# A main tile's 128 partitions ordered by batch first in a streaming dot-product and record-count kernel

## The chip, the cores and the metric

The kernel runs on one core of one Trainium2 chip. The metric is the device time of one execution in microseconds (us). The kernel before takes 630.5 us, the median of two runs (630.48 and 630.51 us).

## The reference

```python
def setup_inputs():
    B, S, D = 8, 2048, 4096
    return {
        "x": np.random.randn(B, S, D).astype(np.float32),
        "w": np.random.randn(D, 1).astype(np.float32),
    }

def reference(x, w):
    proj = (x @ w).squeeze(-1)
    cm = np.maximum.accumulate(proj, axis=1)
    is_record = (proj >= cm).astype(np.float32)
    return np.cumsum(is_record, axis=1).astype(np.float32)
```

Each of the 8 x 2048 rows of x (4096 floats, 16 KiB) is reduced to one dot product with w. Along each batch a running maximum is taken, every position that reaches it counts as a record, and the records are counted up. The input x is 268.4 MB; the output is 64 KiB.

## The kernel before, in words

**Tiles.** The sequence is cut into five groups of N = 384 positions and a rest of 128 positions. A group has NT = 6 main tiles. A main tile holds four batches (`b0` is 0 or 4, alternating with the tile number t) and 128 positions: 512 rows of x, 8 MiB. Each of the 128 partitions gets R = 4 consecutive rows, 64 KiB in one piece. In the kernel before partition p = 4q + b holds rows 4q to 4q + 3 of batch b, so that the batches alternate from one partition to the next (L171 to L173, the pattern "q b (r d)"). Three buffers in SBUF take the tiles in turn (`xbuf`, NS = 3).

**Loads.** All loads of x are issued by SyncE (SP), one after another in the order of the loops at L168. Each main tile is one DMA (L185), but for the last tile of the last group, which is two halves (L178 and L181). A load into a used buffer waits until the tile three places earlier has been consumed (`user_before`, `free`). Behind the main tiles come 13 smaller loads for the rest of 128 positions (L207); their source runs "b i d -> i b d", 32 positions outermost and four batches inside. The 16 KiB of w come by one DMA of 8 partitions from ScalarE's queue (L191). Each group's counts leave by a DMA of 8 partitions (L195), the last ones by L434.

**Compute on a main tile.** VectorE takes the first 2816 columns of each of the four rows of every partition with a fused multiply and sum (L125, in the loop at L270). GpSimd multiplies the remaining 1280 columns of all four rows in one instruction (L291), and ScalarE sums them, row by row (L131). When ScalarE has summed the fourth row the buffer is free. After the six tiles of a group GpSimd adds the two partial sums (L295) and multiplies them with a mask of 128 x 4, `by_b`, that tells which of the four batches a partition holds (L298). TensorE then sorts the sums into rows of batches and columns of positions with 12 matmuls (L335), whose right-hand operand is a mask of 128 x 32, `by_i`, that tells which q a partition holds. VectorE runs the scans on the [8, 384] result (L141, L144, L147) at the head of the next group.

**Masks.** `by_b` and `by_i` are made at the start by two reductions over the identity on VectorE (L249, L253). They also serve the rest of 128 positions, whose partitions alternate batches in the same way (L368, L373, L378). The second reduction signals ScalarE by the semaphore `fo`.

The order on each engine is the order of the program text. Nothing is scheduled by a planner.

Of the kernel before, what the change touches and what calls it, by code (L numbers as in the profile page):

```python
# [13 lines left out]
ALU = mybir.AluOpType  # L14
# [6 lines left out]
def kernel(  # L21
# [16 lines left out]
    P = 128  # L38
# [3 lines left out]
    R = 4  # L42
    NS = 3
    H = 4
    Q = P // H
# [22 lines left out]
    def rows_of(m):  # L68
        return m * H % B, m * H // B * Q
# [9 lines left out]
    def sb(shape, name, **kw):  # L79
        return pool.tile(shape, FP32, name=name, **kw)  # L80

    identity = sb([P, P], "identity")
# [6 lines left out]
    cnt = sb([B, N + P], "cnt")  # L89
    gmask = sb([P, R * NC * B], "gmask")  # L90
    masked = sb([P, 10 * B], "masked")
    fold = sb([P, H + Q], "fold")
    w_v = wpool.tile([P, CV], FP32, name="w_v")
    ps = wpool.tile([P, WC], FP32, name="ps")
    w_row = w2[:NW, :WC]
    by_b, by_i = fold[:, :H], fold[:, H:]

    off = [0]

# [22 lines left out]
    V, A, G, T, SY = nc.vector, nc.scalar, nc.gpsimd, nc.tensor, nc.sync  # L122
# [28 lines left out]
    def at(t):  # L151
        return xbuf[t % NS]

    def user_before(g, t):
        return (t - NS, g + 1) if t >= NS else (t + NT - NS, g)

    def free(u, n):
        return (p7, n) if u == NT - 1 else (fr[u], 2 * n)
# [7 lines left out]
    with tc.tile_critical(no_gpsimd_drain=True):  # L166

        for g in range(NG):  # L168
            for t in range(NT):
                b0, s0 = t % 2 * H, STARTS[g] + t // 2 * P  # L170
                src = x[b0 : b0 + H, s0 : s0 + P, :].rearrange(  # L171
                    "b (q r) d -> q b (r d)", r=R
                )  # L173
                half = R // 2 * D
                last = t == NT - 1
                u, n = user_before(g, t)
                if last and g == NG - 1:
                    i = SY.dma_start(  # L178
                        out=at(t)[:, :half], in_=src[:, :, :half]
                    ).then_inc(xs[t], 16)  # L180
                    SY.dma_start(  # L181
                        out=at(t)[:, half:], in_=src[:, :, half:]
                    ).then_inc(xh, 16)
                else:
                    i = SY.dma_start(out=at(t), in_=src).then_inc(xs[t], 16)  # L185
                    if last:
                        SY.sem_inc(xh, 16)
                if n:
                    i._wait_ge(*free(u, n))
                if g == t == 0:  # L190
                    A.dma_start(  # L191
                        out=w_row, in_=w.rearrange("(k c) one -> k (c one)", k=NW)
                    ).then_inc(ws, 16)
                if t == 4 and g:
                    SY.dma_start(  # L195
                        out=out[:, STARTS[g - 1] : STARTS[g]], in_=cnt[:, :N]
                    )._wait_ge(cs, g + 1).then_inc(od, 16)
# [7 lines left out]
        for i, (m, c0, c1, _, _) in enumerate(TILES):  # L205
            u, xb = slot(m)
            d = SY.dma_start(  # L207
                out=xb[:, c0:c1],
                in_=x[
                    rows_of(m)[0] : rows_of(m)[0] + H,  # L210
                    S0 + rows_of(m)[1] : S0 + rows_of(m)[1] + Q, c0:c1,
                ].rearrange("b i d -> i b d"),
            ).then_inc(xq[i], 16)
# [7 lines left out]
            out=identity, in_=identity, compare_op=ALU.not_equal, fill=1.0,  # L221
# [10 lines left out]
        for n, k in enumerate(order):  # L232
# [3 lines left out]
                out=dst, lhsT=identity[:NW, k : k + 1].to_broadcast([NW, P]),  # L236
                rhs=w_row, start=True, stop=True,
# [12 lines left out]
            out=by_b, in_=identity.rearrange("p (i b) -> p b i", b=H),  # L250
            op=ALU.add, axis=mybir.AxisListType.X,
        )._wait_ge(con, 7)
        V.tensor_reduce(  # L253
            out=by_i, in_=identity.rearrange("p (i b) -> p i b", b=H), op=ALU.add,
            axis=mybir.AxisListType.X,
        ).then_inc(fo, 1)
# [7 lines left out]
        def landed(i, t, j):  # L264
            if j == 0:
                i._wait_ge(xs[t], 16)
            elif t == NT - 1 and j == R // 2:
                i._wait_ge(xh, 16)
# [16 lines left out]
        with G.Fori(0, NG):  # L285
            for t in range(NT):
                rows = at(t).rearrange("p (r d) -> p r d", r=R)
                n = R // 2 if t == NT - 1 else R
                for j in range(0, R, n):
                    xl = rows[:, j : j + n, VC:]  # L290
                    i = G.tensor_mul(  # L291
                        out=xl, in0=xl, in1=w_one.to_broadcast([P, n, PC])
                    ).then_inc(pl, 1)
                    landed(i, t, j)
            G.tensor_tensor(  # L295
                out=sum_t, in0=sum_v, in1=sum_p, op=ALU.add
            )._wait_ge(fr[NT - 1], 2).then_inc(mk, 1)
            G.tensor_tensor(  # L298
                out=gmask.rearrange("p (k b) -> p k b", b=H),
                in0=sum_t.rearrange("p (k o) -> p k o", o=1).to_broadcast(  # L300
                    [P, R * NT, H]
                ),
                in1=by_b.rearrange("p (o b) -> p o b", o=1).to_broadcast(
                    [P, R * NT, H]
                ),
                op=ALU.mult,
            )._wait_ge(mk, 1).then_inc(mk, 1)
            G.wait_ge(pg, 1).then_inc(pg, -1)
# [15 lines left out]
        with T.Fori(0, NG):  # L324
            T.wait_ge(mk, 2).then_inc(p7, 1)
            T.sem_inc(mk, -2)
            T.sem_inc(fr[NT - 1], -2)
            for s in (*xs, xh):
                T.sem_inc(s, -16)
            T.sem_inc(pg, 1)  # L330
            T.wait_ge(od, 16).then_inc(od, -16)  # L331
            for j in range(R):
                for c in range(NC):
                    k = j * NC + c
                    i = T.matmul(  # L335
                        out=ps[:B, c * P + j : (c + 1) * P : R],
                        lhsT=gmask[:, k * B : (k + 1) * B],
                        rhs=by_i, start=True, stop=True,
                    )
                    if k == 0:  # L340
                        i.then_inc(pd, 1)
            i.then_inc(psr, 1)
# [48 lines left out]
        for m in range(B - 2):  # L391
            k = m // 2
            v, p = acc_v[:, m : m + 1], acc_p[:, m : m + 1]
# [16 lines left out]
        for i in range(B - 2, len(TILES)):  # L410
            n = i - (B - 2)
            m, p = TILES[i][0], TILES[i][4]
# [55 lines left out]
```

## Time and profile before

| what | value |
| --- | --- |
| median of the runs before | 630.5 us |
| the profiled execution's own time | 630.45 us |
| its span, first to last instruction | 628.3 us |
| VectorE busy | 406.9 us (65%) |
| GpSimd busy | 360.7 us (57%) |
| ScalarE busy | 171.7 us (27%) |
| TensorE busy | 23.2 us (4%) |
| read from HBM | 268.45 MB |
| DMA rate over the span | 427 GB/s |
| a main load, from issue to landing | 41.7 us (median of 29) |

The profile is one execution. Its span leaves out some 2 us at the ends that the time includes. The profile's page gives each engine's busy time, the span cut into 40 equal slices with the busy share of the 16 DMA engines, the DMA queues with their packets, and the chain of waits: the work that ended last, followed back step by step to what released it. An idle engine that isn't on that chain costs nothing.

### The profile page before, as it was taken

What the parts mean: (1) busy time and instruction counts of PE and PEld (TensorE: products, weight loads), DVE (VectorE), ACT (ScalarE), POOL (GpSimd) and SP (SyncE); (2) the same over time, 40 slices, a digit from 0 to 9 for tenths busy, and PEclk for the clock granted to TensorE, in tenths of its full rate; (3) what the DMA queues carried; (4) which work ended last, traced back from release to release, by engine and by line L of the source; (5) the groups of instructions that cost most, each with busy time, mean ns of one, the idle gap of its engine ahead of it and who ended that gap; (6) DMA issues with size and microseconds to landing.
All of it is one profiled execution on the core that took longest, in us unless ns stands there. A gap on an engine that the chain in (4) does not pass through costs nothing.

```text
span 628.3 us, 1242 instructions
## 1 busy us (share of the span) xinstructions
PE 23.2 (4%) x156; PEld 12.7 (2%) x156; DVE 406.9 (65%) x297; ACT 171.7 (27%) x274; POOL 360.7 (57%) x74
## 2 busy tenths in 40 slices
PE   2600000000000000000000000000000000000000
PEld 1200000000000000000000000000000000000000
DVE  0295775567765557865577566676556875559877
ACT  1033302333113333033330313311333202333344
POOL 0264675455764457744467554576445775449585
DMA  9999999999999999999999999999999999999996
GB/s 390 413 455 413 459 409 459 409 459 409 451 417 417 451 409 459 417 451 426 442 455 414 438 430 442 426 455 413 439 430 442 426 455 413 459 397 430 423 428 267
DMA packets 6434, 268.54 MB, mean 427 GB/s; under 512 B 752, under 2 KB 1040, under 8 KB 1568
## 3 DMA queue, kind: packets, MB, share of 16 engines
q1 hardware_dynamic: 6416, 268.50, 98.9%
q14 instruction: 2, 0.02, 0.0%
q10 hardware_dynamic: 16, 0.02, 0.0%
HBM read 268.45 MB, written 0.07 MB: 427 GB/s over the span
## 4 chain that ended last, share of the span: by engine, by line
DMA 71%; POOL 18%; ACT 7%; issue 2%; DVE 1%; SPq 0%; PE 0%
DMA xall<-in_x_dram 71%; POOL xall L291 18%; ACT xall L131 7%; POOL xall L357 1%; DVE xall L125 0%; SPq L185 0%; PE ps L378 0%; ACT masked L373 0%; SPq L207 0%; POOL masked L368 0%; DVE cm L141 0%; DVE cnt L147 0%; DVE ps L144 0%; SPq L463 0%; DVE small L125 0%
## 5 line engine op out<-in xcount | busy, mean ns | idle before, releaser
L125 DVE CUSTOM_DVE_ANT_0 xall<-xall,w_v 128x2816 f32<-128x2816 f32 (+1 forms) x129 | 385.5, 3041 | 167.7 <-DMA xall<-in_x_dram 167.7
L291 POOL TENSOR_TENSOR xall<-xall,w_sb 128x5120 f32<-128x5120 f32 (+1 forms) x35 | 332.2, 9498 | 242.1 <-DMA xall<-in_x_dram 216.8
L131 ACT ACTIVATE xall<-xall 128x1280 f32<-128x1280 f32 (+2 forms) x130 | 161.3, 1241 | 428.3 <-POOL xall L291 411.3
L335 PE MATMUL ps<-fold,gmask 128*8 128x32 f32 x120 | 7.2, 240 | 563.7 <-PEq L331 563.7
L131 ACT ACTIVATION_READ_ACCUMULATOR xall<-xall 128x1 f32 x130 | 24.2, 186 | 0.0
L357 POOL TENSOR_TENSOR xall<-xall,w_sb 128x1280 f32<-128x1280 f32 (+2 forms) x8 | 21.0, 2629 | 4.4 <-DMA xall<-in_x_dram 2.4
L141 DVE TENSOR_TENSOR_SCAN cm<-ps,cm,small 8x384 f32<-8x384 f32 (+2 forms) x9 | 6.9, 765 | 23.6 <-PE ps L335 23.2
L335 PEld LDWEIGHTS ps<-fold,gmask 128*8 128x8 f32 x120 | 6.5, 114 | 565.9 <-issue 565.9
L257 DVE MEMSET ps<- 8x384 f32 x1 | 0.4, 378 | 24.5 <-ACT w L246 24.5
L235 PE MATMUL w_v<-w,identity 8*128 8x512 f32 x14 | 12.2, 1057 | 0.0
L125 DVE DVE_READ_ACCUMULATOR2_ANT small<- 128x1 f32 x133 | 10.8, 81 | 0.0
L295 POOL TENSOR_TENSOR small<-small 128x24 f32<-128x24 f32 x5 | 1.2, 233 | 13.6 <-ACT xall L131 13.6
L147 DVE TENSOR_TENSOR_SCAN cnt<-ps,cnt,small 8x384 f32<-8x384 f32 (+2 forms) x9 | 6.9, 766 | 0.3
L235 PEld LDWEIGHTS w_v<-w,identity 8*128 8x128 f32 x14 | 4.6, 332 | 7.3 <-issue 7.3
L144 DVE TENSOR_TENSOR ps<-ps,cm 8x384 f32<-8x384 f32 (+2 forms) x9 | 3.9, 435 | 0.3
L243 ACT COPY w_sb<-w_v 128x768 f32<-128x768 f32 x1 | 0.8, 798 | 11.4 <-PE w_v L235 11.4
L125 DVE CUSTOM_DVE_ANT_0 xall<-xall,w_v,small 128x480 f32<-128x480 f32 (+2 forms) x4 | 3.1, 811 | 0.2 <-DVE small L125 0.2
L373 ACT ACTIVATE masked<-fold,small 128x4 f32<-128x4 f32 x10 | 3.0, 297 | 0.3
L378 PE MATMUL ps<-fold,masked 128*8 128x32 f32 x20 | 2.0, 234 | 26.2 <-ACT masked L373 18.2
L242 ACT COPY w_sb<-ps 128x512 f32<-128x512 f32 x1 | 0.6, 585 | 8.5 <-PE ps L235 8.5
L368 POOL TENSOR_TENSOR masked<-fold,small 128x4 f32<-128x4 f32 x8 | 1.6, 203 | 1.6 <-DVE small L125 1.6
L235 PE MATMUL ps<-w,identity 8*128 8x512 f32 x2 | 2.1, 1137 | 11.4 <-DMA w<-in_w_dram 11.4
(20 smaller groups left out, 10.0 us busy)
## 6 DMA issues: line engine op xcount, KB each, us to landing
xall<-in_x_dram SPq DMA_DIRECT2D x6, 2048.0 KB, 31.6
xall<-in_x_dram SPq DMA_DIRECT2D x2, 4096.0 KB, 36.6
xall<-in_x_dram SPq DMA_DIRECT2D x1, 1264.0 KB, 34.0
xall<-in_x_dram SPq DMA_DIRECT2D x1, 816.0 KB, 36.6
xall<-in_x_dram SPq DMA_DIRECT2D x1, 784.0 KB, 35.2
xall<-in_x_dram SPq DMA_DIRECT2D x2, 240.0 KB, 26.2
xall<-in_x_dram SPq DMA_DIRECT2D x29, 41.7
xall<-in_x_dram SPq DMA_DIRECT2D x1, 416.0 KB, 37.0
```

What stands on the lines that cost most here:

```text
L125: return V.tensor_tensor_reduce(out=xsl, in0=xsl, in1=wsl, scale=1.0, scalar=seed, op0=ALU.mult, op1=ALU.add, accum_out=dst,)
L131: return A.activation(out=xsl, in_=xsl, func=ACTF.Copy, accum_out=dst)
L141: V.tensor_tensor_scan(out=cm_, data0=src, data1=low, initial=cm0, op0=ALU.max, op1=ALU.max,)._wait_ge(psr, base).then_inc(psr, 1)
L144: V.tensor_tensor(out=src, in0=src, in1=cm_, op=ALU.is_ge)._wait_ge(psr, base + 1).then_inc(psr, 1)
L147: V.tensor_tensor_scan(out=cnt_, data0=src, data1=low, initial=cnt0, op0=ALU.add, op1=ALU.max,)._wait_ge(psr, base + 2).then_inc(cs, 1)
L235: i = T.matmul(out=dst, lhsT=identity[:NW, k : k + 1].to_broadcast([NW, P]), rhs=w_row, start=True, stop=True,).then_inc(bw, 1)
L291: i = G.tensor_mul(out=xl, in0=xl, in1=w_one.to_broadcast([P, n, PC])).then_inc(pl, 1)
L335: i = T.matmul(out=ps[:B, c * P + j : (c + 1) * P : R], lhsT=gmask[:, k * B : (k + 1) * B], rhs=by_i, start=True, stop=True,)
L357: G.tensor_mul(out=xl, in0=xl, in1=w_pool(*p))._wait_ge(xq[i], 16).then_inc(pl, 1)
L368: return eng.tensor_tensor(out=e, in0=by_b, in1=acc.to_broadcast([P, H]), op=ALU.mult)
L373: return A.activation(out=e, in_=by_b, func=ACTF.Copy, scale=acc)._wait_ge(pa, na).then_inc(ms, 1)
L378: return T.matmul(out=ps[:B, k * Q : (k + 1) * Q], lhsT=masked[:, n * B : (n + 1) * B], rhs=by_i, start=start, stop=stop,)
```

## The change

The source pattern of a main tile becomes "b q (r d)": batch outermost, then q, then the 64 KiB piece. Partition p = 32b + q now holds rows 4q to 4q + 3 of batch b. Two further masks, `in_b` (128 x 4) and `in_q` (128 x 32), tell batch and q in this order; two reductions more on VectorE make them at the start, and the mask of a group (L298) and the right-hand operand of its matmuls (L335) use them in place of `by_b` and `by_i`. The loads of the rest of 128 positions, their masks, and all sizes and waits stay as they were.

```diff
-    fold = sb([P, H + Q], "fold")
+    fold = sb([P, 2 * (H + Q)], "fold")
...
-    by_b, by_i = fold[:, :H], fold[:, H:]
+    by_b, by_i = fold[:, :H], fold[:, H : H + Q]
+    in_b, in_q = fold[:, H + Q : 2 * H + Q], fold[:, 2 * H + Q :]
...
                 src = x[b0 : b0 + H, s0 : s0 + P, :].rearrange(
-                    "b (q r) d -> q b (r d)", r=R
+                    "b (q r) d -> b q (r d)", r=R
                 )
...
         V.tensor_reduce(
+            out=in_b, in_=identity.rearrange("p (b q) -> p b q", b=H), op=ALU.add,
+            axis=mybir.AxisListType.X,
+        )
+        V.tensor_reduce(
+            out=in_q, in_=identity.rearrange("p (b q) -> p q b", b=H), op=ALU.add,
+            axis=mybir.AxisListType.X,
+        )
+        V.tensor_reduce(
             out=by_i, in_=identity.rearrange("p (i b) -> p i b", b=H), op=ALU.add,
             axis=mybir.AxisListType.X,
         ).then_inc(fo, 1)
...
-                in1=by_b.rearrange("p (o b) -> p o b", o=1).to_broadcast(
+                in1=in_b.rearrange("p (o b) -> p o b", o=1).to_broadcast(
...
-                        rhs=by_i, start=True, stop=True,
+                        rhs=in_q, start=True, stop=True,
```

## The prediction, written before the changed kernel ran

> **What bounds the kernel now.** I read the page's slices and its DMA part first, then the chain of waits, then a window over three tiles in the steady part.
>
> ```profile
> span 628.3 us, 1242 instructions
> ...
> DMA  9999999999999999999999999999999999999996
> ...
> DMA packets 6434, 268.54 MB, mean 427 GB/s; under 512 B 752, under 2 KB 1040, under 8 KB 1568
> ...
> q1 hardware_dynamic: 6416, 268.50, 98.9%
> ...
> q10 hardware_dynamic: 16, 0.02, 0.0%
> ```
>
> The 16 DMA engines are busy in every slice but the last. The loads of x are the bound, and all of them are on one queue.
>
> Pieces of the chain of waits, in order of time (start us, us, what):
>
> ```profile
> 42.97 11.06 POOL xall L291
> 54.03 0.02 issue
> 54.05 0.04 ACT xall L131
> 54.10 1.13 issue
> 55.23 3.95 ACT xall L131 x7
> 59.18 0.02 issue
> 59.20 41.71 DMA xall<-in_x_dram
> 100.91 0.07 issue
> 100.98 11.06 POOL xall L291
> ```
>
> This is one buffer's round: load, GpSimd, ScalarE, load again, 58.01 us, and it carries three tiles. The chain shows GpSimd in it, but the DMA engines don't stop meanwhile, as the window over that round shows (columns: stretch, length, busy us of each engine, clock, DMA share, GB/s):
>
> ```profile
> core 0: us, PE busy (x) PEld busy (x) DVE busy (x) ACT busy (x) POOL busy (x), PEclk, DMA share, GB/s
> 43.00:101.00 58.00, 0.00 (x0) 0.00 (x0) 36.35 (x25) 15.75 (x26) 33.13 (x4) 1.00 1.00 434
> ```
>
> A DMA share of 1.00 at 434 GB/s: while one tile is consumed, two others are queued. Each engine moves 434/16 = 27.1 GB/s. A tile has 128 pieces of 64 KiB, 8 per engine; three tiles in 58.01 us make 2.417 us a piece. The 30 main tiles take 240 x 2.417 = 580.1 us. All else in the span (first bytes, the smaller loads, the last scans) is 628.3 - 580.1 = 48.2 us.
>
> **What the page tells of how a load is spread.** Every engine that takes part in a DMA ends its share with a small packet. The kernel has 31 main loads and 13 smaller ones into 128 partitions, 5 stores of 8 partitions and w's load of 8. 44 x 16 + 5 x 8 + 8 = 752, the page's count under 512 B. The queue of w's load, q10, has 16 packets: 8 rows and 8 endings. So the loads into 128 partitions run on 16 engines and those of 8 rows on 8 only.
>
> **What the Trainium skill says.**
> - "DMA: Bandwidth & Descriptors", section "Why a DMA increments its semaphore by 16 and not by 1": the number of engines k is the largest up to 16 that divides the slowest dimension (of size over 1) of both source and destination, and on SP's queue these are the lowest-numbered k. The counts above agree: 128 against 32 gives 16, 8 against 8 gives 8.
> - The same page, "Rules for kernel authors": an outermost dimension of size c under 16 confines the whole DMA to at most c engines. No load of before shows a c of 4.
> - The same page, "The descriptor swizzle": a 128-partition transfer on 16 engines gives each one the 8 partitions of one SBUF port. The even 27.1 GB/s per engine fits.
> - "SBUF — State Buffer", section "Door 1: The DMA port swizzle (why `[64,N]` ≈ `[32,N]`)": 16 ports of 8 partitions; partition p and p + 32 share a port, p and p + 64 don't. A port is worth 27.2 GB/s, and partitions 0 to 63 reach 196 GB/s where 0 to 127 reach 328 (1 MiB). No stretch of before has two streams held to one port, so the trace is silent on it.
>
> **The change part by part.**
>
> 1. *Two reductions more on VectorE.* L249 took 377 ns and L253 277 ns: 0.65 us in all. Behind them VectorE sits idle 24.5 us for ScalarE's copy of w (L257), so nothing is added there. The signal `fo` comes 0.65 us later to ScalarE, which then waits 8.5 us for TensorE. If the cover were gone: 0.65 us.
> 2. *Other masks in L298 and L335.* The same shapes and counts, 5 instructions of 345 ns and 120 of 240 ns: 0.
> 3. *The 31 main loads.* The pieces stay 64 KiB and 128 per tile, with the same bytes, issues and waits. What changes is the slowest dimension of the source: 32 (q) becomes 4 (b). With a destination of 128 the largest common k is 4. Engine e then takes batch e, 32 pieces in place of 8, into partitions 32e to 32e + 31; 12 engines get nothing. Whether an engine gets faster when others rest, no stretch of before shows; 10% would be the most I could argue from rates that stand so still, and I keep 27.1 GB/s, since one figure for all sixteen at once speaks for a limit of each engine's own path. Main pieces per engine: 30 x 32 = 960, at 2.417 us: 2320.4 us, in place of 580.1.
> 4. *The ports.* Engine 0 walks partitions 0 to 31 and engine 1 walks 32 to 63, from the same moment, at the same speed: p and p + 32, the same port, all the way. Likewise engines 2 and 3. If a port is worth one engine's rate, each pair shares 27.1 GB/s and a piece takes 4.834 us: 960 x 4.834 = 4640.8 us. What the pair gains is its stagger: the leader enters the next port (4 pieces, 262 KB) alone. In the trace's packet records the first sixteen pieces of before start within 0.42 us of each other, 11 KB or 4% of a port's stretch. With fair sharing the stagger is kept and doesn't grow. It gives back 4% of the second 2320.4: 93 us.
> 5. *Who waits.* SP's loads wait for ScalarE to free a buffer (435.5 us in 22 waits at L185 now). GpSimd's 11.06 us and ScalarE's 5.1 us per tile stay; two tiles of over 77 us each are queued meanwhile, so these hide, and engines 0 to 3 never run dry. w's load has rows on engines 0 to 3 behind slower pieces: some us later, but the first tile itself lands over 50 us later still.
> 6. *The 13 smaller loads* keep 32 outermost and 16 engines. Engines 4 to 15 do their share early; engines 0 to 3 do theirs behind the main pieces, the same bytes per engine as now. The 48.2 us stay.
>
> Sum of the likeliest case, against the profiled execution: 4640.8 - 93 + 48.2 = 4596 us of span. The time stood 2.15 us above the span (630.45 against 628.3), and the median of the runs at 630.5: 4598 us, say 4600.
>
> **Rivals.**
>
> *Four engines, but no collision* (the port isn't the limit, or unfair sharing soon pulls a pair apart by 4 pieces, after which each has a port to itself): 2320.4 + 48.2 + 2.15 = 2371 us. For it: w's eight rows (q10) wrote to partitions 0 to 7 while x streamed to the same ports, and in the packet records they took 84 ns each and the pieces beside them at most 30 ns more than usual. Against it: 2 KB may vanish in a buffer, and the skill's table of ports. Chance 0.28.
>
> *Collision for part of the run* (the stagger grows slowly until the pair is apart): between the two; half of the run makes about 3485 us. Chance 0.15.
>
> *The loads keep 16 engines* (the rule doesn't apply to this form: the split is taken from the 128 partitions, or the two outer dimensions are cut anew). Then part 3 falls, only the hidden 0.65 us is left, and the time is 630.5 us, not slower. It turns on one thing: whether the generator looks at the source's slowest dimension. For it: the two sides of before differ (128 and 32) and still gave 16, so the counts alone don't prove that the smaller rules. Against it: the rule names both sides. Chance 0.04.
>
> *A third limit*: four streams whose addresses lie 32 MiB apart slow one another in HBM. Nothing in the trace shows it, since batches with that distance are read now at 434 GB/s. It would lie above 4720 or, without the ports, between 2400 and 3000; chance 0.02.
>
> **How the numbers follow.** Collision all the way has 0.51, and is the forecast: 4600 us. Its own range runs from 4250 (a stagger of 15 to 20% of a port's stretch) to 4720 (no stagger, and some lost time). With the partial case 0.66 is held. To leave out no more than 2 in 10 the range must reach the no-collision case, which is narrow, at 2371. So 2330 to 4720. About 2% is what a measurement of this kernel can tell from no change. Slower by over 2%: 0.95 (0.51 + 0.28 + 0.15 + most of the third limit). Within 2%: 0.04. Faster: 0.01, since the bytes and the rate of 16 busy engines leave nothing to gain.
>
> **What would show it.** Step 3: the DMA share of the slices falls to about a quarter, and the packets under 512 B fall from 752 by 31 x 12 = 372 to 380. If they stay at 752, the step is wrong. Step 4: the rate in a steady window is some 55 GB/s and a load into a buffer lands some 155 us after the one before it; 108 GB/s and 77 us show the first rival. Step 5: GpSimd and VectorE wait for DMA almost all the time, and SP's wait for ScalarE remains. Step 6: the smaller loads still take 16 engines, and the last 40 us run near 108 GB/s or less, as only engines 0 to 3 have work left. The prediction is wrong at its root if the engine count stays at 16, and wrong by a factor of two in the added time if ports don't collide.

## The result, and the profile after

The changed kernel takes 2713.9 us (two runs, 2713.90 and 2713.91), against 630.5 us: 4.30 times as long, 95% interval 4.29 to 4.32. The profiled execution took 2713.91 us with a span of 2711.8 us. That is 1886 us less than the forecast of 4600, inside the range, and in the case that had 0.15, collision for part of the run.

From the page of the changed kernel, first the lines that answer to those of before, then the rate in the 40 slices of 67.8 us:

```profile
span 2711.8 us, 1244 instructions
...
DMA  2222222222222222222222222222222222222463
GB/s 55 55 60 63 63 67 67 71 74 79 82 92 102 107 108 110 108 108 108 110 108 108 108 108 108 108 108 108 110 108 108 108 110 108 108 108 108 138 175 113
DMA packets 6062, 268.54 MB, mean 99 GB/s; under 512 B 380, under 2 KB 668, under 8 KB 1196
...
q1 hardware_dynamic: 6044, 268.50, 26.9%
q10 hardware_dynamic: 16, 0.02, 0.0%
```

The DMA share of a slice is 2 tenths where it was 9 or more, and the small packets under 512 B are 380, as 31 loads on 4 engines instead of 16 make them: 752 - 31 x 12. The queue q1 moved the same 268.50 MB in 26.9% of the 16 engines' time: a quarter of them, all the time. The GB/s line holds the rest of the story. It begins at 55, climbs for 13 slices and stays at about 108 from some 900 us on.

Three windows of the same kernel, at the start, on the slope and after it (columns as before: stretch, length, busy us of the engines, clock, DMA share, GB/s):

```profile
core 0: us, PE busy (x) PEld busy (x) DVE busy (x) ACT busy (x) POOL busy (x), PEclk, DMA share, GB/s
20.00:140.00 120.00, 13.15 (x16) 4.65 (x14) 2.94 (x4) 2.06 (x3) 0.00 (x0) 1.00 0.25 56
...
640.00:760.00 120.00, 0.00 (x0) 0.00 (x0) 12.12 (x8) 5.12 (x8) 11.05 (x1) 1.00 0.25 84
1000.00:1120.00 120.00, 0.00 (x0) 0.00 (x0) 24.24 (x16) 10.24 (x16) 22.09 (x2) 1.00 0.25 109
```

The DMA share is 0.25 in all three: four engines are busy from first to last, and never more than four. Only what they move doubles. So the slope is not a lack of work for them; each busy engine moves 14 GB/s at first and 27 in the end.

Pieces of the chain of waits in the steady part (start us, us, what):

```profile
2323.72 0.07 issue
2323.79 11.05 POOL xall L300
2334.83 66.15 another core or an unknown queue
2400.99 0.07 issue
2401.05 11.05 POOL xall L300
```

A tile every 77.26 us (2401.05 - 2323.79), 32 pieces of 2.414 us. The "unknown queue" is the load itself, which the chain couldn't match to its issue in this run: the waits of the same trace put 2326.0 us of GpSimd's idle time down to loads of x, where it was 216.8 us before. GpSimd's multiplication is the same 11.05 us as before.

### The profile page after: what moved, and what is told of

Same layout as the page of the kernel before. It is cut to its first block, busy times and chain, and to the rows that moved or that the text cites. A ratio compares the mean times of both kernels' runs of the same rounds, so it can differ in the third digit from the quotient of the medians.

```text
span 2711.8 us, 1244 instructions
## 1 busy us (share of the span) xinstructions
PE 23.2 (1%) x156; PEld 12.7 (0%) x156; DVE 408.0 (15%) x299; ACT 171.7 (6%) x274; POOL 360.7 (13%) x74
## 3 DMA queue, kind: packets, MB, share of 16 engines
q1 hardware_dynamic: 6044, 268.50, 26.9%
## 5 line engine op out<-in xcount | busy, mean ns | idle before, releaser
L300 POOL TENSOR_TENSOR xall<-xall,w_sb 128x5120 f32<-128x5120 f32 (+1 forms) x35 | 332.2, 9497 | 2326.0 <-DMA xall<-in_x_dram 2326.0
## 6 DMA issues: line engine op xcount, KB each, us to landing
xall<-in_x_dram SPq DMA_DIRECT2D x1, 784.0 KB, 60.3
```

The lines of the kernel that those rows point to most:

```text
L300: i = G.tensor_mul(out=xl, in0=xl, in1=w_one.to_broadcast([P, n, PC])).then_inc(pl, 1)
```

## The experiments

Packet records of the trace give each piece's start and length. On 2 or 4 engines the pieces of one engine can be told by following one another without a gap. The **lead** below is the difference between the pieces that two paired engines have moved. Every kernel is the changed kernel with the edit shown, in short form: where a tile comes by several loads, the loop over them stands as a comment, and the counts that follow from the number of loads are left out. In the kernels with two, four or eight loads a tile the last tile isn't halved either. The masks were timed 12 times and the last kernel four times, all others once; so the readings rest on the rates and packet records as well as on the times.

**The masks alone.**

```diff
-                    "b (q r) d -> b q (r d)", r=R
+                    "b (q r) d -> q b (r d)", r=R
```

> The two new reductions and the new masks alone; the main loads keep the pattern of before, so the masks sort the sums by the wrong partitions and the output is not the reference's. Both theories (ports, or streams 32 MiB apart in HBM) put the whole cost into the loads: 630.5 us, ratio 1.000, 752 packets under 512 B. If the masks cost anything, it is at most the 0.65 us of the reductions.

Measured: 630.32 us against 630.33 in the same rounds, ratio 1.000, interval 0.999 to 1.001. The reductions and masks cost nothing; the whole loss is in the pattern of the loads.

**Streams that never walk at equal offsets.**

```diff
+                step = S * D - (5 * R * D + D + 1024)
+                src = bass.AP(
+                    tensor=src.tensor, offset=src.offset,
+                    ap=[[step, H], [R * D, Q], [1, R * D]],
+                )
```

> As the changed kernel, but the four streams of a load start 32 MiB less 340 KiB apart (5 pieces of 64 KiB, one row and 4 KiB less), so that they never walk at the same offset; it sums other rows than the reference asks for. Partitions, engines (4) and bytes stay. Port theory: unchanged, the slices start at 55 to 60 GB/s and rise to 108 by about 900 us, some 2714 us in all (2650 to 2780). HBM theory (equal offsets 32 MiB apart slow one another): 108 GB/s from the first slice, some 2400 us.

Measured: 2732.8 us. The rate in its slices:

```profile
GB/s 54 54 58 60 63 61 68 68 75 78 84 91 98 107 110 109 108 109 109 108 108 110 109 108 108 109 109 108 109 109 109 108 109 109 108 108 109 138 173 105
```

The same slope from 54 to 108. The distance of the streams in HBM is not what holds them. That rival falls.

**Two engines on one port, and on two.** Each tile comes by two loads of 64 partitions, so that only engines 0 and 1 work. In the first kernel a load covers 64 neighbouring partitions, in the second every second one.

```diff
-                    i = SY.dma_start(out=at(t), in_=src).then_inc(xs[t], 16)
+# one port:  two loads, h = 0, 1
+                    i = SY.dma_start(out=at(t)[h * 64 : h * 64 + 64], in_=src[2 * h : 2 * h + 2])
+# two ports: two loads, h = 0, 1
+                    i = SY.dma_start(out=at(t)[h:P:2], in_=src[2 * h : 2 * h + 2])
```

> As the changed kernel, but each main tile comes by two loads of two batches and 64 partitions: 2 engines by the rule, and engines 0 and 1 walk partitions p and p + 32, the same port. Port theory: 27 GB/s at first, 54 once one is 4 pieces ahead; 1920 pieces an engine at 2.417 us make 4641 us, plus 48, plus 313 us of collisions as in the changed kernel, plus about 35 at the end: 5035 us (4950 to 5120). HBM theory: the same time as the kernel whose two engines walk p and p + 64.

> As the one with two loads a tile, but each load writes every second partition, so that engine 0 walks 0 to 62 and engine 1 64 to 126: p and p + 64, never the same port. Sources, engines (2) and bytes as there; the partitions hold other rows than the masks say, so the output is not the reference's. Port theory: every piece 2.418 us from the second one on, 54 GB/s throughout, 4641 + 48 + 35: about 4725 us, some 310 less than its twin. HBM theory: no difference between the two (within 30 us).

Measured: 5020.7 us and 4722.3 us. The rate in the slices of the first:

```profile
GB/s 28 30 32 34 37 42 51 54 54 54 54 54 54 54 54 54 54 54 54 54 54 54 54 54 54 54 54 54 54 54 54 54 54 54 54 54 54 54 116 88
```

and of the second:

```profile
GB/s 54 54 54 54 54 54 54 54 54 54 54 54 54 54 54 54 54 54 54 54 54 54 54 54 54 54 54 54 54 54 54 54 54 54 54 55 54 58 118 92
```

Windows over the same stretch of both, first p and p + 32, then p and p + 64 (columns as before):

```profile
20.00:140.00 120.00, 13.43 (x16) 4.65 (x14) 2.94 (x4) 2.06 (x3) 0.00 (x0) 1.00 0.12 28
```

```profile
20.00:140.00 120.00, 5.05 (x6) 1.39 (x5) 2.94 (x4) 1.47 (x2) 0.00 (x0) 1.00 0.13 55
```

A share of 0.12 to 0.13 is two engines of 16 in both. Sources, bytes, pieces and engines are the same. With p and p + 32 the two engines together move one engine's worth, 28 GB/s, and climb to 54; with p and p + 64 they move 54 from the first slice. Of the 298 us between the two, the packet records put 286 and 297 us (on the two engines) into pieces longer than 2.418 us in the first half of the run. This is the direct evidence for the ports. What it tests of the Trainium skill's map of them ("SBUF — State Buffer", "Door 1: The DMA port swizzle (why `[64,N]` ≈ `[32,N]`)"), that p and p + 32 share a port and p and p + 64 don't, holds here. The second kernel also takes every second partition, so it changes port after 2 pieces and not 4; the next kernel has that too, with p and p + 32, and starts at 31 GB/s.

The lead in the first of the two, from its packet records:

```
pieces moved by the leader   5.5   14.0   31.5   65.1   116   175   209   249   290   622
lead, pieces                0.24   0.38   0.64   1.14  1.84  2.92  3.45  3.95  3.94  3.95
```

It grows in a straight line, 0.0154 pieces per piece, and stops dead just short of 4, where the leader leaves a port as the other enters it. The two pairs of the changed kernel also come to rest at 3.94.

**A change of port after every two pieces.**

```diff
+# four loads, h = 0, 1 and o = 0, 1
+                    i = SY.dma_start(out=at(t)[h * 64 + o : h * 64 + 64 : 2], in_=src[2 * h : 2 * h + 2, o::2])
```

> As the kernel with two loads a tile whose engines 0 and 1 share ports (5021 us), but every load takes every second partition, four loads a tile: the two engines change port after 2 pieces and not 4. There the lead grew by 0.0154 pieces with each piece, 0.061 with each change of port, until it stood at 3.95 pieces, and 298 us were lost against the twin on different ports (4722 us). If a change of port makes the lead grow, it grows twice as fast and 2 pieces are enough: 65 pieces, some 80 us lost, about 4800 us. If it grows with the bytes: 130 pieces, some 155 us, about 4880 us. In both, the lead should come to rest at 2 pieces. If ports had nothing to do with it, 5021 us.

Measured: 4793.0 us, 71 us above the kernel without collision. The rate in its slices:

```profile
GB/s 31 49 55 54 55 54 55 55 54 55 54 55 55 54 55 54 55 55 54 55 54 55 55 54 55 54 55 55 54 55 54 55 55 54 55 54 55 68 104 90
```

The lead is 0.30 after 5.7 pieces, 1.00 after 25.7, 1.89 after 52.4, and rests at 1.95. Growth per piece has doubled, per change of port it has stayed near 0.061 to 0.069 pieces (about 4 KB). So it is the change of port that moves the pair apart, not the sharing between changes. The number of loads has doubled too, so the border between two loads is a rival; the packet records rule it out. Once both engines are under way, until the pair is nearly apart, the follower starts each stretch later behind the leader than the stretch before, by 0.13 to 0.19 us in both kernels, inside a load as at its end (0.13 to 0.17 us there).

**A lead from the start.** The first tile comes by loads of few partitions, which run on the lowest-numbered engines only.

```diff
+                if g == t == 0:
+                    parts = [(k, k + 1) for k in range(4)]
+                    parts += [(4 + 3 * k, 7 + 3 * k) for k in range(4)]
+                    parts += [(16, 32), (32, 64), (64, 96), (96, 128)]
+                    for p0, p1 in parts:
+                        SY.dma_start(
+                            out=at(t)[p0:p1],
+                            in_=src[p0 // Q, p0 % Q : p0 % Q + p1 - p0],
+                        ).then_inc(xs[t], 16)
```

> As the changed kernel, but the very first tile comes by 12 smaller loads (four of 1 partition, four of 3, one of 16, three of 32) that give engine 0 four pieces of 64 KiB more than engine 1 and engine 2 four more than engine 3; 29 tiles follow as in the changed kernel. Port theory with a lead of 4 pieces that lasts: 108 GB/s from about 50 us on, every later piece 2.418 us until the smaller loads at the end; 29 x 32 + 15 pieces on engine 0 at 2.417 us make 2279 us, plus 48 us, plus the 35 us that the main pieces lost beside the smaller loads, plus 2: about 2365 us. If the slow start has another cause (a warm-up, HBM pages): still rising slowly from 55 GB/s, about 2690 us.

Measured: 2414.9 us, 299 less than the changed kernel. The rate in its slices of 60.3 us:

```profile
GB/s 139 71 104 109 109 109 109 108 109 109 109 108 109 109 109 109 109 109 109 109 109 109 109 109 109 109 109 109 109 109 109 109 109 108 109 109 109 158 178 111
```

From the third slice on it stands at 104 to 109: four engines and no collision. The 50 us over the estimate lie mainly in the first two slices; the middle half of the first 128 pieces took 5.1 to 8.1 us each. My estimate left out that the loads of the first tile meet on ports as well. A load of 32 neighbouring partitions reaches 8 ports by the map above, one of 16 reaches 4. On 16 engines that is two or four engines to a port, and by an estimate from 2.418 us a piece then takes 4.8 or 9.7 us.

**The smaller loads held back.**

```diff
+        SY.wait_ge(p7, NG)
```

> As the changed kernel, but SP issues the 13 smaller loads only when the last group has been consumed. In the changed kernel the main pieces on engines 0 to 3 lost 35 us while engines 4 to 15 did their part of the smaller loads. Theory that the two mix badly (any shared way): the halves of the last main tile take 1.213 us a piece and the pieces of the smaller loads 0.611 us; the main loads end 35 us earlier, but the smaller loads start some 17 us (GpSimd and ScalarE on the last tile, the matmuls) after that, and 39 us plus 5 us follow: about 2700 us. Theory that the smaller loads themselves are slow after a load on 4 engines: they stay at 1.25 us a piece, and the time is 2735 us or more.

Measured: 2686.3 us, 28 less than the changed kernel and 14 below my estimate; 6 of these because the smaller loads start 11 us after the last main piece, not 17. The halves of the last tile take 1.213 us a piece now, all of them, and nine in ten of the 16 KiB pieces between 0.611 and 0.625; in the changed kernel the halves take up to 2.58, and half of the 16 KiB pieces 1.245 or more. The two windows that show it, of this kernel:

```profile
core 0: us, PE busy (x) PEld busy (x) DVE busy (x) ACT busy (x) POOL busy (x), PEclk, DMA share, GB/s
2560.00:2600.00 40.00, 0.00 (x0) 0.00 (x0) 7.84 (x6) 7.73 (x12) 6.32 (x2) 1.00 0.25 108
...
2632.00:2672.00 40.00, 2.19 (x32) 1.72 (x32) 22.82 (x20) 12.12 (x21) 19.82 (x15) 1.00 0.85 353
```

and of the changed kernel in the stretch where both kinds run:

```profile
core 0: us, PE busy (x) PEld busy (x) DVE busy (x) ACT busy (x) POOL busy (x), PEclk, DMA share, GB/s
2610.00:2640.00 30.00, 0.00 (x0) 0.00 (x0) 6.10 (x4) 2.62 (x4) 5.61 (x1) 1.00 0.73 177
```

A share of 0.73 but 177 GB/s: about 12 engines busy on average, at 15 GB/s each in place of 27. Kept apart, neither kind of load is slow. The two mix badly, and mixing costs more than the wait.

**Eight engines, together and apart.** Eight batches in a tile make the slowest dimension 8; the second kernel adds an uneven first tile.

```diff
-                src = x[b0 : b0 + H, s0 : s0 + P, :].rearrange(
+                src = x[:, STARTS[g] + t * 64 : STARTS[g] + t * 64 + 64, :].rearrange(
...
+# apart only: the first tile
+                    for b, ks in enumerate([(2, 6, 2, 6)] * 2 + [(16,)] * 6):
+                        p0 = 0
+                        for k in ks:
+                            SY.dma_start(
+                                out=at(t)[16 * b + p0 : 16 * b + p0 + k],
+                                in_=src[b, p0 : p0 + k],
+                            ).then_inc(xs[t], 16)
+                            p0 += k
```

> Batch first with all eight batches in a tile and 64 positions of each: the slowest dimension of the source is 8, so 8 engines; engine e walks 16 partitions, and e and e + 2 meet on ports. The masks still speak of four batches, so the output is not the reference's. Engine count alone: 480 x 2.417 + 50 = 1210 us. Port theory with the growth of the lead seen in the changed kernel (about 4.2 KB at each change of port, so 4 pieces after some 61 changes, 244 pieces): 313 us more and some of the 35: 1524 to 1560 us, slices rising from 110 to 217 GB/s. Collision all the way: 2370 us.

> The kernel with eight batches in a tile on 8 engines (2241 us), but its first tile comes by 14 loads (four of 2 partitions, four of 6, six of 16) that give engines 0 and 1 four pieces more than 2 and 3, and 4 and 5 four more than 6 and 7. The output is not the reference's, as there. Port theory: 217 GB/s once the first tile is past, pieces 2.418 us; 8 + 6 + 29 x 16 = 478 pieces, 1155 us, plus 48, plus some 50 us for the start and the mixing at the end: 1210 to 1290 us. If 8 engines are held by something else: above 2000 us.

Measured: 2240.8 us and 1336.8 us. The rate in the slices of the first:

```profile
GB/s 104 105 108 103 108 108 105 108 103 110 109 107 111 108 111 113 116 112 118 112 116 118 116 117 119 119 116 119 122 128 122 129 131 124 132 129 136 163 199 163
```

and of the second, whose slices are 33.4 us:

```profile
GB/s 95 106 84 192 218 218 220 220 212 214 218 220 220 214 214 218 218 220 220 212 214 218 220 220 212 214 220 218 220 218 214 214 218 220 220 212 190 190 190 49
```

The first was a miss. I had carried over the growth of the lead from four engines, and with eight it is several times slower: the mean piece of a tile falls only from 5.00 to 4.0 us by the last tile before the smaller loads mix in. The second shows that nothing but the pairs holds eight engines: 217 GB/s, pieces of 2.418 us. It lies 47 us above my interval. The first tile lands only after 96 us, in three slices of 95, 106 and 84 GB/s, and its pieces took 9.5 us on the mean; that is the crowding of the first tile again, 16 engines on 4 ports, by an estimate worth 4 x 27.1 = 108 GB/s.

**Sixteen engines, batch first.** Loads of single batches restore 16 engines, but 32 partitions of one batch reach 8 ports by the map above.

```diff
+# alternate: four loads a tile
+                for b in (0, 2, 1, 3):
+                    i = SY.dma_start(out=at(t)[b * Q : (b + 1) * Q], in_=src[b])
+# together: eight loads a tile; apart: the same, and the first tile by 12 loads
+                for h in (0, 1):
+                    for b in (0, 2, 1, 3):
+                        i = SY.dma_start(out=at(t)[b * Q + h : (b + 1) * Q : 2], in_=src[b, h::2])
+# apart, first tile
+                    for k in (1, 15, 16, 3, 13, 16, 5, 11, 16, 7, 9, 16):
...
```

> Batch first with one load per batch of 32 partitions, in the order of batches 0, 2, 1, 3 of the tile: 16 engines by the rule, two partitions each, engines 2i and 2i + 1 on one port, and after each load of two pieces the other half of the ports. Engine count alone: 630 to 640 us. Port theory: a lead of 2 pieces parts a pair. If the lead grows by 4.2 KB at each change of port: 31 changes of 2 pieces, 62 pieces at half rate on average half the time, 75 us more: about 705 us. If it grows by 1.6% of each piece: 125 pieces, 151 us more: about 781 us. No growth: 1200 us.

> The twin: the same 8 loads a tile for all 30 tiles, nothing that parts the pairs. Port theory: the pairs stay together, as on 16 engines with four loads a tile (1256 us), where the lead did not grow: 1230 to 1260 us, pieces about 5.0 us. If changing ports after every piece parts the pairs after all: 700 us or less.

> Batch first on 16 engines, with the pairs parted from the start. A main tile comes by 8 loads of 16 partitions (every second partition of a batch; batches 0, 2, 1, 3), so that an engine changes between the halves of the ports with each piece of 64 KiB; the first tile comes by 12 loads of 1, 15, 16, 3, 13, 16, 5, 11, 16, 7, 9 and 16 partitions, which give each even engine one piece more than the odd one beside it. Port theory: each piece 2.418 us and 430 GB/s once the first tile is past; engine 0 has 12 + 29 x 8 = 244 pieces, 590 us, plus 48 and some 10 us for the uneven first tile and the mixing at the end: 640 to 670 us. Theory that many loads of few partitions are slow in themselves: above 1100 us, as its twin without the uneven first tile.

Measured: 1255.6 us, 1230.0 us and, for the third, 807.2 us in the profiled execution and 812.6, 848.0 and 867.3 in three more. From the page of the kernel "together":

```profile
DMA  9999999999999999999999999999999999999997
GB/s 206 207 237 205 205 207 237 205 205 207 237 205 205 207 237 205 205 216 228 205 205 231 213 205 205 237 207 205 207 236 207 205 231 213 205 205 237 207 321 295
```

and "apart":

```profile
DMA  9998999999999999999999999999999999999981
GB/s 122 137 107 153 212 345 332 365 365 391 374 381 365 365 365 365 365 378 387 381 365 365 365 404 378 365 387 394 362 368 404 378 410 397 397 398 206 316 372 58
```

In both the 16 engines are busy nearly all the time until the end. Busy is not fast: in the first of these pages they move some 205 to 237 GB/s until the smaller loads, about 8 ports' worth (8 x 27.1 = 217). In neither of the first two kernels did the lead grow to speak of, as far as the pieces tell (5.0 us from start to end with four loads, 4.91 at the start and 4.87 at the end with eight), so my numbers for "alternate", 705 or 781, were both wrong, and 1200, "no growth", was right. The third parts the pairs, and the rate rises to some 365 to 410 GB/s. Its time is a miss, above my 640 to 670: nearly all pieces take some 2.8 us in the middle of the run and not 2.418, so that the rate falls short of 430 GB/s, and the first tile, crowded like the two above, lands only at 97 us. No version came out ahead of the kernel before, which has all 16 engines at 434 GB/s.

## Why the prediction was right, and where it was wrong

The prediction named what happened, "the stagger grows slowly until the pair is apart", but as its third case, at 0.15. The range holds the result because it was stretched down to the case without collision; the likeliest case with its own range, 4250 to 4720, missed it by far.

*Steps 1 and 2, masks and reductions at nothing*: shown by the run with the masks alone.

*Step 3, four engines in place of 16*: shown by the packets (380), the DMA share (0.25) and the steady 77.26 us a tile. Its 2320.4 us for 960 pieces stands, and so does one engine's rate: with 12 others at rest a piece takes the same 2.418 us. The rule of the Trainium skill that I rested this on ("DMA: Bandwidth & Descriptors", "Why a DMA increments its semaphore by 16 and not by 1") is confirmed for k of 4 by the changed kernel's count; the loads of 64 partitions from two batches ran on two engines, by the share of 0.12 to 0.13.

*Step 4, the ports*: the mechanism was right and the size wrong. The pairs do collide, and at the start a piece took 4.75 us on the mean of the first 124, near my 4.834. The sentence that failed is "With fair sharing the stagger is kept and doesn't grow". It grows by about 0.06 pieces at each change of port, and after about 240 pieces out of 960 the pair is 4 pieces apart for good. The term of the sum was 2320.4 - 93 = 2227 us. In the packet records of the changed kernel the slowest engine's pieces lost 313 us to it. I had the two ends of this step, 0 and 2227, and the trace of before couldn't say which; what I lacked was any number for how two streams on one port shift against each other.

*Step 5, who waits*: SP's wait for ScalarE's release remained, and the four engines never ran dry:

```profile
SPq L186 <- ACT xall L132: 1832.2, 22, 170.2
```

22 waits as before, with 1832.2 us in place of 435.5. They cost nothing, since the DMA share holds at 0.25 across all the windows above.

*Step 6, the smaller loads*: mis-sized by 35 us. I had them follow at no cost to the main pieces. While engines 4 to 15 did their share early, the busy engines ran at little over half rate on average, by the window above; the slowest engine's main pieces lost 35 us there. What came after its last main piece took 39 us, as it did before (2666.9 to 2706.3 us). The run with these loads held back shows the cause to be the mixing.

The sum as it should have been: 2320.4 + 313 + 35 + 48.2 = 2716.6 us, against a span of 2711.8.

*The rivals*: 16 engines kept, and a limit in HBM, are both ruled out. "No collision" was the wrong account of the first 900 us and the right one of the rest. w's eight rows that took 84 ns each, which I counted for it, said nothing on two long streams; whether they were too small to show a shared port, no run tells.

## What to carry to other kernels

Look at the slowest dimension of both sides of a load: their largest common divisor up to 16 was the number of DMA engines at work on the main loads in the runs here (2, 4, 8 and 16), and reordering partitions can change it without changing one byte. Then look at which partitions the engines write at the same moment: two engines on p and p + 32 moved one engine's worth in this case, on p and p + 64 twice that, and a busy DMA row doesn't tell the difference, only GB/s per busy engine does. If a pair can't be parted by layout, a lead of one port's stretch at the start parted it for good with four and eight engines; with sixteen it brought 365 to 410 GB/s, less than the layout of the kernel before. And a first tile cut into loads of few partitions pays for it: 16 engines then crowd on 4 or 8 ports.

## What the runs showed of the hardware that was not expected

- Two streams on one port drift apart by about 4 KB at each change of port (0.061 to 0.069 pieces of 64 KiB, stretches of 4 and of 2 pieces) and come to rest at one stretch less 0.05 pieces (3.95 and 1.95), with two engines; four engines rest at 3.94. Why the leader gains there is not settled. Nor is why the gain is several times smaller with eight engines and next to none with sixteen: no run told these apart.
- Two kinds of load on the same engines and ports can slow one another more than the ports explain. While main loads on four engines and smaller loads ran together, nine in ten of the 16 KiB pieces took over 1.0 us, and most of them 1.2 to 1.3, where they take 0.611 alone. If each of the other twelve engines keeps to one port, which no run here tests, the four walking engines can stand in the way of four of them at most at one moment. With the pairs parted on 16 engines nearly all pieces took the same 2.8 us. The cause of both is not settled.
